# A bias tile with its own place, four transpose tiles, a third raw buffer and an earlier weight load in a hybrid S5 and chunked-attention layer

## The chip, the cores and the metric

The kernel runs on one core of a Trainium2 chip. Its time is the device time of one execution in microseconds; the kernel before has a median of 2287.17 us over three runs (2282.82 to 2289.53). All data are float32. Large products are made as three products of operands that are split into a high and a low part ("hi" and "lo", type float32r).

The engines go by their short names: PE (TensorE, the matrix products), DVE (VectorE), ACT (ScalarE), POOL (GpSimd) and SP (SyncE, which issues most DMAs). Each engine takes its instructions in order. A DMA is issued by SP or by POOL and carried by the core's 16 DMA engines; a wait that stands before a DMA's issue holds up everything behind it on the issuing engine.

## The reference

One layer of a trunk with two parallel head groups over 2048 tokens and 1024 channels:

```python
h = rmsnorm(x, norm_mix_g)
proj = h @ w_in                      # u_ssm | q | k | v, 512 columns each
y_ssm = s5_mixer(u_ssm, ...)         # 32 groups of 16 channels, 64 complex states each, GLU
y_att = chunked_attention(q, k, v, rel_bias)   # 8 heads of 64, own chunk of 64 and 8 before it
mixed = concat(rmsnorm(y_ssm, g_ssm), rmsnorm(y_att, g_att))
x = x + mixed @ w_out
h2 = rmsnorm(x, norm_ffn_g)
x = x + (silu(h2 @ w_gate) * (h2 @ w_up)) @ w_down
return rmsnorm(x, norm_final_g)
```

The attention adds a learned bias to each score, `bias[h, clip(key - query, -128, 128)]`, masks keys outside the band, and takes the softmax. The S5 group is a diagonal complex state-space scan: discretised transition powers, input matrix and output matrix are worked out from the parameters, then the states are scanned along time.

## The kernel before

The work runs in stages: the projection of the S5 input `u` (`u_phase`, until about 110 us) with the scan's parameters (`ssm_prologue`) beside it; the attention with the S5 scan and then the mixing stage between its steps (`att_phase`); the rest of the mixing stage; gate and up; down. The change touches the seam from the first stage to the second.

**Order.** PE's matmuls and transposes are kept in the order in which the program writes them (`Ordered`). The instructions issued through `k.V`, `k.A` and `k.Q` (DVE, ACT, SP) keep their order among one another (`Pinned`). All others are placed by a planner at compile time: it takes the earliest written instruction that is ready in its own estimate of time, so that on SP or POOL a later written DMA can pass one that isn't ready. The order that it gives to each engine is then fixed, and the semaphore waits are made to fit.

**The seam.** In the order of the program:

- `u_phase` forms four blocks of `u` (groups of 24 matmuls `ps<-hi,wuh`), takes them out of PSUM into `us` tiles (`evac`, four buffers), and POOL stores these (`u<-us`, L517). Before the last block it calls `front[0]`, which starts the first query/key unit `qk_unit(0, 0)` and thereby loads weights 0 and 4, and after its first group `front[1]` (`operands`): `hT_unit(0)` loads and normalises the first 512 tokens, and `table` builds the bias table.
- The bias table `nbm` lies in DRAM: for each of 8 heads 128 rows of 640 values. SP issues one copy from DRAM to DRAM (`nbms<-nbs`, 2560 KB), in which each row is shifted by one value against the one above, and then two stores of a corner of 1e30 (`nbms<-corner`) for keys outside the band.
- The prologue then makes its pool `pk`: `bbg` (loaded from DRAM in pieces of 16 values, 64 bytes), four `vg` tiles, `kt`, and the tiles `bst`. With `bbg` and `vg` PE makes 64 small matmuls (`pp<-vg,bbg`), and after them 32 transposes (`transposes`), two to a PSUM tile `pp` (six buffers); ACT copies each into a `bst` tile, and POOL stores each of the four blocks (`bsts<-bst`, L319).
- Before these 64 matmuls PE runs the query/key product of the first head pair (`pf<-hi,w`), after the transposes the steps of the attention: scores (`sc`), the value product of the first half of the heads (`v_unit(0, 0)`, weights 8 and 10), the next pair's product `qk_unit(0, 1)` (weights 1 and 5), and the scan's units (`ssm_unit`).
- A weight of the first 512 tokens is loaded into a `raw` buffer and split into a `w` tile (three buffers) by ACT (hi, L177) and DVE (lo, L178); `keep_w` stores the split weight to DRAM for the later tokens (`wss<-w`).
- A score is taken from PSUM by one DVE instruction that adds the bias tile `nb` of its head and takes the minimum (L863). The first head's `nb` is loaded by SP where its first score is written, that of each next head at the third score of the one before.

**Memory.** The tiles of a pool lie upward from its lower end in the order in which they are first used. Of the pools on the right side, `aw` (the attention's operands and weights) lies at the end of memory, `uo` (the second set of operands, hi0o, lo0o, hi1o, ... of 2,048 bytes per partition, 32,768 in all) under it, and `u1` (the weights of `u`, small tiles, three `pb`, four `us`) under that. When `u_phase` ends, `pk` is laid where `uo` and `u1` were, with its upper end at the lower end of `aw`: five `kt` of 4,096 bytes, `bbg` 2,048, `dm` 2,048, four `vg` of 4,096, two `bst` of 4,096. A tile waits, one by one, for the last use of the tiles whose bytes it takes.

Of the kernel before, what the change touches and what calls it, by code (L numbers as in the profile page):

```python
# [16 lines left out]
P = 128  # L17
# [3 lines left out]
NG, CH, NS = 32, 16, 64  # L21
# [88 lines left out]
def f32(ap):  # L110
    return ap.bitcast(F32)
# [63 lines left out]
def split(k, hi, lo, raw, lo_eng=None, hi_eng=None):  # L175
    nc = k.nc
    (hi_eng or nc.scalar).copy(hi, raw)  # L177
    (lo_eng or nc.gpsimd).tensor_tensor(lo, raw, f32(hi), op=ALU.subtract)  # L178


def ssm_prologue(k, ident, S):

    tc, nc, io = k.tc, k.nc, k.io
    V = nc.vector
    with tc.tile_pool(name="pro", bufs=1) as p:
# [122 lines left out]
                eng.tensor_tensor(out, t1, t2, op=op)  # L308

        def transposes(pk, b_, wt):  # L310
            bst = k.t(pk, "bst", [P, 8, 2, NS], bufs=2)
            for q in range(4):
                ps = k.t(k.pro_psum, "pp", [P, 512])[:].rearrange("p (a b) -> p a b", a=4)
                for c in range(2):
                    k.te.transpose(ps[:, c, :], wt[c][:, q].rearrange("p j c -> p (j c)"), ident[:])
                nc.scalar.copy(bst[:, 2 * q : 2 * q + 2].rearrange("p g c n -> p c g n"), ps[:, :2].rearrange("p c (g n) -> p c g n", g=2))
                if q % 2:
                    yield
            nc.gpsimd.dma_start(S["bst"][b_], bst[:].rearrange("p g c n -> p (g c n)"))  # L319
# [82 lines left out]
        pk = k.pk()  # L402
# [26 lines left out]
        for b_ in range(4):  # L429
            yield from transposes(pk, b_, wts[b_])  # L430
# [267 lines left out]
def att_phase(k, ident, S):  # L698
    tc, nc, io = k.tc, k.nc, k.io
    with ExitStack() as cx:  # L700
        aw = tc.alloc_tile_pool(name="aw", reuse_waits="tile", bufs=1, side="right")
        hT, vts, qk, keep = {}, {}, {}, {}

        def load_w(sb, n):

            w = k.t(aw, "w", [P, 2, 1024], F32R, bufs=WB)
            if sb == 0:
                raw = k.t(aw, "raw", [P, 1024], bufs=2)
                pin = n in (0, 4)
                (k.Q if pin else nc.sync).dma_start(raw[:], io["w_qk"][n] if n < 8 else io["w_v"][n - 8])  # L710
                split(k, w[:, 0], w[:, 1], raw[:], k.V if pin else k.wlo_eng, k.A if pin else None)
                keep[n] = w
            else:
                nc.sync.dma_start(f32(w[:]), S["ws"][n])
            return w[:, 0], w[:, 1]
# [5 lines left out]
        def hT_unit(sb, q0=0, q1=KT):  # L721
            hi, lo = hT.setdefault(sb, ([], []))
            ts = slice(sb * SB, (sb + 1) * SB)
            xts = {}
            V, A, Q = (k.V, k.A, k.Q) if sb == 0 else (nc.vector, nc.scalar, nc.sync)

            def load(q):
                if q < q1:
                    x = RING[q] if sb == 0 and q < 2 * DB else None
                    xts[q] = k.t(aw, x, [P, SB]) if x else k.t(aw, "xt", [P, SB], bufs=XB)  # L730
                    Q.dma_start(xts[q][:], io["xt"][q * P : (q + 1) * P, ts])

            ahead = 2 if sb else KT
            for q in range(q0, q0 + ahead):
                load(q)
            def low(q):
                V.tensor_tensor(lo[q][:], xts[q][:], f32(hi[q][:]), op=ALU.subtract)

            for q in range(q0, q1):
                yield  # L740
                load(q + ahead)
                xt = xts[q]
                for v, n in zip(hT[sb], ("hi", "lo")):
                    v.append(k.t(aw, f"{n}{q}x" if q < DB and sb % 2 else f"{n}{q}", [P, SB], F32R))
                V.scalar_tensor_tensor(xt[:], xt[:], k.gm[:, q : q + 1], S["rsn"][:, ts], op0=ALU.mult, op1=ALU.mult)
                A.copy(hi[q][:], xt[:])  # L746
                if sb == 0 and q:
                    low(q - 1)
                if sb or q == KT - 1:
                    low(q)  # L750
            yield

        def qk_unit(sb, pr):
            ws = [load_w(sb, n) for n in (pr, 4 + pr)]
            yield
            hi, lo = hT[sb]
# [42 lines left out]
        def v_unit(sb, fh):  # L799
            ws = [load_w(sb, 8 + 2 * r + fh) for r in range(2)]  # L800
            yield
            for i in range(4):
                vts[4 * sb + i, fh] = k.t(pv, f"v{fh}", [P, H // 2, 2 * HD], F32R)
            hi, lo = hT[sb]
            for i in range(4):
                ps = k.t(pfs, "pf", [P, 256])
                ic = slice(i * P, (i + 1) * P)
                for q in range(KT):
                    cs = slice((q % 4) * 256, (q % 4 + 1) * 256)
                    wh, wl = (w[:, cs] for w in ws[q // 4])  # L810
                    k.ta.matmul(ps[:], hi[q][:, ic], wh, start=q == 0, stop=False)
                    k.ta.matmul(ps[:], hi[q][:, ic], wl, start=False, stop=False)
                    k.ta.matmul(ps[:], lo[q][:, ic], wh, start=False, stop=q == KT - 1)
                    if q % 2 and q < KT - 1:
                        yield
                if i == 0:
                    for r in range(2):
                        keep_w(8 + 2 * r + fh)
                vt = vts[4 * sb + i, fh]
                pv3 = ps[:].rearrange("p (h d) -> p h d", h=4)  # L820
                nc.scalar.copy(vt[:, :, :HD], pv3)
                nc.vector.tensor_tensor(vt[:, :, HD:], pv3, f32(vt[:, :, :HD]), op=ALU.subtract)
                yield
# [3 lines left out]
        class Head:  # L827
            pass

        nbs = {}  # L830

        def load_nb(h):
            nb = k.t(aa, "nb", [P, 640], bufs=2)
# [88 lines left out]
        def table():  # L922
            corner = k.t(aw, "corner", [64, 64])
            nc.gpsimd.memset(corner[:], 1e30)
            k.Q.dma_start(S["nbm"][:], bass.AP(S["nb"].tensor, S["nb"].offset + 1, [[768, H], [1, P], [1, 640]]))
            for m in range(2):
                k.Q.dma_start(S["nbm"][:, m * 64 : m * 64 + 64, m * 576 : m * 576 + 64].rearrange("h p c -> p h c"), corner[:].unsqueeze(1).to_broadcast([64, H, 64]))

        def operands():
            for _ in hT_unit(0):  # L930
                pass
            table()

        pro = u_phase(k, ident, S, aw, (lambda: next(first), operands))
        pfs = cx.enter_context(tc.tile_pool(name="apf", bufs=2, space=bass.MemoryType.PSUM, reuse_waits="tile"))
        pps = k.pro_psum = tc.alloc_tile_pool(name="apro", bufs=6, space=bass.MemoryType.PSUM, reuse_waits="tile")
# [711 lines left out]
def block_kernel(tc, io, phases="pusamf"):  # L1648
# [3 lines left out]
    with ExitStack() as cx:  # L1652
# [32 lines left out]
        with tc.tile_pool(name="powers", bufs=1) as p:  # L1685
            S["a8"] = k.t(p, "a8", [P, 2, NPR, 16])
            S["sw"] = k.t(p, "sw", [P, 3, 2, NPR])
            mix = att_phase(k, ident, S)
# [58 lines left out]
```

## Time and profile before

| | us |
|---|---|
| median of three runs | 2287.17 |
| the profiled execution | 2284.15 |
| its span, first to last instruction | 2282.4 |
| PE busy in the span | 2180.3 |
| first query/key product ends, 64 small matmuls begin | 121.24 |
| first score | 141.29 |
| second pair's query/key product begins | 160.08 |

A row of the timeline gives start and duration in us, engine, line of the kernel, operation, output and inputs by the program's names, the count of instructions merged into it, and in brackets the idle time of the engine before it with what ended it. A row of the waits gives who waited for whom, then total time, number and longest. A row of a table of stretches gives for each engine (PE, PEld, DVE, ACT, POOL) the busy time and in brackets the instructions, then the granted clock of PE as a share of full speed, the busy share of the DMA engines and GB/s. A row of the DMA issues gives the transfer, its count, KB each, and the median time from issue to landing.

### The profile page before, as it was taken

How to read it: one execution, taken by the hardware profiler on the slowest of the kernel's cores; microseconds unless marked ns; L12 is line 12 of the kernel's file. 1: busy time of each engine (PE TensorE's matmuls, PEld its weight loads, DVE VectorE, ACT ScalarE, POOL GpSimd, SP SyncE). 2: the span in 40 equal slices, each digit the busy share in tenths (PEclk: the TensorE clock that was granted, in tenths of full speed). 3: DMA queues.
4: the chain of work that ended last, by engine and by line, in shares of the span. 5: the costliest groups of instructions: out<-in, count | busy, mean ns of one | idle time of the engine just before them, and what ended most of it. 6: DMA issues, size and time to landing. Idle time of an engine off the chain costs nothing.

```text
span 2282.4 us, 30410 instructions
## 1 busy us (share of the span) xinstructions
PE 2180.3 (96%) x10576; PEld 1833.1 (80%) x10576; DVE 1480.2 (65%) x2253; ACT 999.0 (44%) x1686; POOL 1011.1 (44%) x1222
## 2 busy tenths in 40 slices
PE   8978899999997999999999999999999999999998
PEld 6767688898986788878888887788888878888887
DVE  7845555656548656776776659776646376579576
ACT  6335555555557552343333334433333343345322
POOL 3406645456651122145555555555555414345450
PEclk9989999999998999999999999999999999999999
DMA  8787776766645334844454557454523297565552
GB/s 300 262 285 264 221 219 192 217 201 194 198 129 172 134 124 149 281 157 152 162 193 161 205 187 269 152 209 165 175 88 120 75 334 266 173 212 194 184 212 75
DMA packets 215890, 437.26 MB, mean 192 GB/s; under 512 B 27448, under 2 KB 58216, under 8 KB 208632
## 3 DMA queue, kind: packets, MB, share of 16 engines
q1 hardware_dynamic: 209736, 417.74, 55.2%
q0 software_dynamic: 6000, 17.58, 2.4%
q8 instruction: 83, 1.36, 0.2%
q14 instruction: 71, 0.58, 0.1%
HBM read 294.98 MB, written 132.41 MB: 187 GB/s over the span
## 4 chain that ended last, share of the span: by engine, by line
PE 77%; DVE 8%; issue 5%; DMA 4%; POOL 3%; ACT 2%; SPq 1%; DVEq 0%; POOLq 0%; ACTq 0%
PE ps L77 20%; PE X L77 18%; PE Y L77 9%; PE big L77 9%; PE pf L77 8%; PE W L77 4%; PE pj L77 4%; PE pt L80 2%; PE sc L77 2%; DMA xt<-in_xt 1%; DVE lo L178 1%; SPq L579 1%; DVE S L1407 1%; DVE acc L1617 1%; DVE cm L91 0%
## 5 line engine op out<-in xcount | busy, mean ns | idle before, releaser
L77 PE MATMUL X<-hi,c 128*128 128x512 f32 x1408 | 452.3, 392 | 6.0 <-ACT u L1425 3.3
L77 PE MATMUL ps<-hd,hd 128*128 128x512 f32 (+1 forms) x1968 | 428.2, 379 | 2.0 <-DVE hd L178 2.0
L77 PEld LDWEIGHTS ps<-hd,hd 128*128 128x128 f32 x1968 | 356.4, 188 | 72.4 <-DVE hd L178 3.1
L178 POOL TENSOR_TENSOR c<-S,c 128x512 fp32r<-128x512 f32 x172 | 249.4, 1452 | 263.1 <-ACT c L177 259.1
L77 PEld LDWEIGHTS X<-hi,c 128*128 128x128 f32 x1408 | 265.8, 189 | 64.4 <-ACT u L1425 5.3
L77 PE MATMUL X<-lo,c 128*128 128x512 f32 x704 | 275.4, 391 | 0.0
L178 POOL TENSOR_TENSOR hd<-hd 128x1536 fp32r<-128x1536 f32 (+1 forms) x46 | 156.3, 3401 | 216.1 <-ACT hd L177 204.6
L177 ACT CAST hd<-hd 128x1536 fp32r<-128x1536 f32 (+1 forms) x106 | 147.2, 1393 | 215.8 <-DMA hd<-hq 158.0
L178 POOL TENSOR_TENSOR c<-raw,c 128x512 fp32r<-128x512 f32 x129 | 184.2, 1428 | 128.2 <-ACT c L177 95.5
L77 PE MATMUL Y<-hi,c 128*128 128x512 f32 x704 | 225.6, 390 | 7.7 <-DVE u L1429 7.7
L1556 DVE TENSOR_TENSOR acc<-acc,ps 128x512 f32<-128x512 f32 x196 | 129.2, 681 | 75.0 <-PE ps L77 74.7
L77 PE MATMUL big<-m,woh 128*128 128x512 f32 x512 | 162.8, 400 | 0.0
L77 PEld LDWEIGHTS Y<-hi,c 128*128 128x128 f32 x704 | 132.5, 188 | 37.4 <-DVE u L1429 9.8
L177 ACT CAST c<-S 128x512 fp32r<-128x512 f32 x176 | 109.4, 622 | 115.3 <-PE Y L77 56.5
L77 PE MATMUL pf<-hi,w 128*128 128x512 f32 x416 | 150.9, 415 | 7.1 <-ACT hi L746 3.7
L77 PEld LDWEIGHTS X<-lo,c 128*128 128x128 f32 x704 | 133.0, 189 | 27.6
L1425 ACT COPY u<-X 128x512 f32<-128x512 f32 x132 | 77.2, 585 | 169.7 <-PE X L77 169.7
L863 DVE CUSTOM_DVE_ANT_0 s<-sc,nb 128x640 f32<-128x640 f32 (+4 forms) x128 | 94.4, 738 | 84.8 <-PE sc L77 80.7
L617 POOL TENSOR_TENSOR st<-X,a 128x128 f32<-128x128 f32 (+2 forms) x136 | 46.8, 344 | 231.3 <-ACT X L603 193.0
L177 ACT CAST c<-raw 128x512 fp32r<-128x512 f32 x132 | 82.1, 622 | 139.8 <-PE Y L77 78.6
L178 DVE TENSOR_TENSOR hd<-hd 128x1536 fp32r<-128x1536 f32 (+1 forms) x60 | 117.9, 1966 | 34.0 <-ACT hd L177 33.3
L77 PE MATMUL Y<-lo,c 128*128 128x512 f32 x352 | 137.3, 390 | 0.0
(468 smaller groups left out, 4605.0 us busy)
## 6 DMA issues: line engine op xcount, KB each, us to landing
w<-wss SPq DMA_DIRECT2D x36, 1024.0 KB, 5.9
hq<-g SPq DMA_DIRECT2D x133, 256.0 KB, 2.1
hd<-hq SPq DMA_DIRECT2D x42, 768.0 KB, 4.6
hd<-wc SPq DMA_DIRECT2D x42, 768.0 KB, 6.0
raw<-in_w_gate SPq DMA_DIRECT2D x44, 512.0 KB, 3.7
raw<-in_w_up SPq DMA_DIRECT2D x44, 512.0 KB, 4.0
wc<-px SPq DMA_DIRECT2D x66, 256.0 KB, 3.5
wss<-w SPq DMA_DIRECT2D x12, 1024.0 KB, 5.4
```

The lines of the kernel that those rows point to most:

```text
L77: return self.tc.keep_in_program_order(self.tc.nc.tensor.matmul(*a, **b))
L80: return self.tc.keep_in_program_order(self.tc.nc.tensor.transpose(*a, **b))
L177: (hi_eng or nc.scalar).copy(hi, raw)
L178: (lo_eng or nc.gpsimd).tensor_tensor(lo, raw, f32(hi), op=ALU.subtract)
L579: ins = nc.sync.dma_start(out, in_)
L617: eng.tensor_tensor(t[:, :, :, :n], src, ar, op=ALU.mult)
L863: nc.vector.tensor_tensor_reduce(s[:, :nk].rearrange("p (a b) -> p a b", a=nch), ps[:, :nch, :half], hd.nb[:, nk - 1 :: -1].rearrange("p ( ...
L1407: V.tensor_tensor(o[:], x, y, op=op)
L1425: nc.scalar.copy(u[:], ps[:])
L1556: V.tensor_tensor(a, a, ps[:], op=ALU.add)
L1617: nc.vector.scalar_tensor_tensor(v, v, k.go[:, i : i + 1], rs, op0=ALU.mult, op1=ALU.mult)
```

## The change

- `transposes` gets four `bst` buffers in place of two.
- `raw` gets three buffers in place of two, and its loads get a function of their own, `load_raw`. In `operands`, SP now issues the loads of weights 8 and 10 ahead of the bias table, and that of weight 1 between the table's copy and its two corner stores. All three are kept in SP's written order; before, they were placed by the planner where the weights are split.
- The first head's bias tile gets a place of its own, `nb0`, in a pool at the left side that lives as long as the attention, and is loaded by POOL right behind the table. The other heads' tiles are loaded as before.

```diff
         def transposes(pk, b_, wt):
-            bst = k.t(pk, "bst", [P, 8, 2, NS], bufs=2)
+            bst = k.t(pk, "bst", [P, 8, 2, NS], bufs=4)
...
         hT, vts, qk, keep = {}, {}, {}, {}
+        nb0 = k.t(cx.enter_context(tc.tile_pool(name="nb0", bufs=1)), "nb0", [P, 640])
+        raws = {}
+        def load_raw(n, dma):
+            raw = raws[n] = k.t(aw, "raw", [P, 1024], bufs=3)
+            dma(raw[:], io["w_qk"][n] if n < 8 else io["w_v"][n - 8])
...
             if sb == 0:
-                raw = k.t(aw, "raw", [P, 1024], bufs=2)
                 pin = n in (0, 4)
-                (k.Q if pin else nc.sync).dma_start(raw[:], io["w_qk"][n] if n < 8 else io["w_v"][n - 8])
+                if n not in raws:
+                    load_raw(n, (k.Q if pin else nc.sync).dma_start)
+                raw = raws.pop(n)
...
-        nbs = {}
+        nbs = {0: nb0}
...
             k.Q.dma_start(S["nbm"][:], bass.AP(S["nb"].tensor, S["nb"].offset + 1, [[768, H], [1, P], [1, 640]]))
+            load_raw(1, k.Q.dma_start)
             for m in range(2):
                 k.Q.dma_start(S["nbm"][:, ...], corner[:]...)
...
             for _ in hT_unit(0):
                 pass
+            for n in (8, 10):
+                load_raw(n, k.Q.dma_start)
             table()
+            nc.gpsimd.dma_start(nb0[:], S["nbm"][0])
```

The pool `pk` thereby takes 57,344 bytes per partition in place of 49,152, and `aw` 4,096 more.

## The prediction

> **What bounds the kernel now.** I read the page first, then the waits of PE in the stretch that the diff touches, then that stretch in order of time on each engine, and last the landing times of its transfers. The page says that PE is the bound over the whole:
>
> ```profile
> span 2282.4 us, 30410 instructions
> PE 2180.3 (96%) x10576; PEld 1833.1 (80%) x10576; DVE 1480.2 (65%) x2253; ACT 999.0 (44%) x1686; POOL 1011.1 (44%) x1222
> PE 77%; DVE 8%; issue 5%; DMA 4%; POOL 3%; ACT 2%; SPq 1%; DVEq 0%; POOLq 0%; ACTq 0%
> ```
>
> PE is idle for some 102 us in all (2282.4 - 2180.3), and its matmuls run in the order written. Time is won only where PE waits or runs slowly, and what is won early stays won while nothing behind it is tied to a fixed moment. Between 120 and 420 us it has three single waits over 3 us. Two lie in the stretch of the change and stand in brackets below; the third lies behind it, at 184 us (total, times, longest):
>
> ```profile
> PE pf L77 <- ACT w L177: 3.4, 1, 3.4
> ```
>
> In order of time on PE, from the end of the first query/key product to the start of the second:
>
> ```profile
> 121.24 7.27 PE L77 MATMUL pp<-vg,bbg 128*16 128x128 f32 x64
> 128.44 3.68 PE L80 MATMUL pp<-ident,vw 128*128 128x128 f32 x28
> 139.25 1.11 PE L80 MATMUL pp<-ident,vw 128*128 128x128 f32 x4 [7.13 <-ACT bst L316]
> 141.29 0.48 PE L77 MATMUL sc<-hi2x,hi0x 128*128 128x128 f32 x1 [0.93 <-ACT bst L316]
> ...
> 151.11 0.55 PE L77 MATMUL sc<-hi2x,hi0x 128*128 128x256 f32 x1 [4.21 <-DVE mn L863]
> ...
> 157.12 0.48 PE L77 MATMUL pf<-w,hi 128*128 128x256 f32 x2
> ...
> 160.08 0.40 PE L77 MATMUL pf<-hi,w 128*128 128x512 f32 x1
> ```
>
> From 121.24 to 160.08 PE spends 38.84 us. The 7.13 us wait is the third transpose tile: ACT stands before it until the first tile's store has landed. The 4.21 us wait is the first score, which needs its bias table:
>
> ```profile
> 129.43 2.21 ACT L316 COPY bst<-pp 128x256 f32<-128x256 f32 x8
> ...
> 138.82 0.92 ACT L316 COPY bst<-pp 128x256 f32<-128x256 f32 x3 [4.50 <-DMA bsts<-bst]
> ```
>
> ```profile
> 150.67 0.29 DVE L863 CUSTOM_DVE_ANT_0 s<-sc,nb 128x128 f32<-128x128 f32 x1 [2.89 <-DMA nb<-nbms]
> ```
>
> Both waits also cost clock. In these stretches of 2 us the third value from the right is the granted clock of PE:
>
> ```profile
> 132.00:134.00 2.00, 0.12 (x2) 0.00 (x0) 0.00 (x0) 0.72 (x1) 0.47 (x1) 1.00 1.04 371
> 136.00:138.00 2.00, 0.00 (x0) 0.00 (x0) 0.00 (x0) 0.00 (x0) 0.00 (x0) 0.54 1.03 413
> 146.00:148.00 2.00, 0.91 (x6) 0.70 (x5) 0.42 (x1) 0.37 (x1) 0.00 (x0) 0.90 0.94 233
> ```
>
> PE stops at about 132.1, is at half clock from about 136, and is back at about 146.4, some 7 us after it went on at 139.25. After the second wait it went on at 151.11, and the full-speed group of value products begins at 157.1, some 6 us later.
>
> **The change part by part.** What it can remove, first. At full clock the same stretch needs: the 64 small matmuls, 7.2 us (121.24 to 128.44); 32 transposes at 3.68/28 = 0.131 us, 4.2; the gap from the last transpose to the first score, which waits for the last bst copies to free the PSUM bank, 0.9; three scores with three groups of 24 value matmuls. One such group at full clock ran from 157.12 to 160.08, 2.96 us, with its scores before it about 0.35, so 3 x 3.3 = 9.9. Together 22.2. So at most 38.84 - 22.2 = 16.6 us can go: 7.1 by the four transpose tiles, 4.2 by the early bias tile, 5.3 by the clock and small gaps.
>
> *Four transpose tiles* remove the 4.50 us wait of ACT and with it PE's 7.13, since four blocks then have four tiles. What is late next is PSUM: six buffers, emptied by ACT at 2.21/8 = 0.28 us for two transposes (0.26 us of PE), so they keep step.
>
> *The bias tile by POOL.* Before, it stands on SP behind two weight stores that wait for a split:
>
> ```profile
> 93.22 0.80 SPq L91 DMA_DIRECT2D nbms<-nbs  x1
> 106.22 0.39 SPq L408 DMA_DIRECT2D bbg<-bbs  x1
> 106.93 9.58 SPq L415 DMA_DIRECT2D vg<-vs  x1
> 116.61 1.37 SPq L91 DMA_DIRECT2D nbms<-corner  x2
> 118.19 3.35 SPq L415 DMA_DIRECT2D vg<-vs  x3
> 121.59 2.00 SPq L91 DMA_DIRECT2D wss<-w  x2
> 123.63 2.31 SPq L710 DMA_DIRECT2D raw<-in_w_v  x2
> ...
> 135.61 6.68 SPq L719 DMA_DIRECT2D wss<-w  x2
> 142.38 0.72 SPq L834 DMA_DIRECT2D nb<-nbms  x1
> ```
>
> On POOL it waits only for the two corner stores (issued by 118 us, landing 4.4 us later by the row below). With one more landing, 8 us at the busy place where it now stands, it is there at about 131, ahead of any first score.
>
> ```profile
> nbms<-corner SPq DMA_DIRECT2D x2, 128.0 KB, 4.4
> ```
>
> ```profile
> nb<-nbms SPq DMA_DIRECT2D x1, 320.0 KB, 8.0
> ```
>
> It costs one POOL issue of about 0.5 us. What queues behind it on POOL are the kt and bst stores, from 127 us on, so this is covered if the planner puts it after the `us` stores (else see the third rival).
>
> *Third raw buffer, and the three weight loads moved.* The value weights (8, 10) now go ahead of the bias table, weight 1 (the second pair's query weights) between table and corners. SP loses 2.31 us of issue at 123.63. The value weights were loaded behind the first weight stores; now they come some 30 us earlier, so with the other waits gone they aren't the next stall. Their price is 1.5 MB more in the rings before the corners, of which 1 MB stands ahead of the table. At the 219 GB/s of the next row (last value) that is up to 4.8 us of delay for the table and the corners:
>
> ```profile
> 100.00:110.00 10.00, 10.00 (x44) 8.04 (x43) 9.91 (x17) 3.80 (x7) 0.56 (x2) 1.00 0.65 219
> ```
>
> The corners were issued at 116.61 only because the issue of the first vg took 9.58 us, so that delay is largely hidden; uncovered it would move vg 2 to 4, which land just in time now, by as much.
>
> *What the larger bst moves in memory.* This is the term that speaks against the change. `pk` lies directly under `aw`, where `uo` and `u1` lay. By the sizes in the code it was 49,152 bytes per partition and becomes 57,344, and its tiles are laid upward from its lower end. Before, bbg begins 28,672 bytes below the end of `pk`: that is hi1o. It waits for the second q of the last `us` group, and is issued at 106.22, vg one q (three matmuls, 0.7 us) later, as the rows show. After, bbg begins 36,864 below: above the 32,768 bytes of `uo`, in the four `us` tiles at the end of `u1`. It must then wait until a `us` tile has been stored. These rows are POOL's first three stores of the last group, and the landings of issues from 105 to 112 us:
>
> ```profile
> 109.38 1.74 POOL L517 DMA_DIRECT2D u<-us  x3 [10.46 <-DVE us L91]
> ```
>
> ```profile
> u<-us POOLq DMA_DIRECT2D x4, 256.0 KB, 5.1
> vg<-vs SPq DMA_DIRECT2D x1, 512.0 KB, 13.6
> bbg<-bbs SPq DMA_DIRECT2D x1, 256.0 KB, 11.8
> ```
>
> The quickest vg load (minimum, median and maximum of four) and the weight stores:
>
> ```profile
> DMA to landing us min/median/max: 4.9/5.6/13.6
> ```
>
> ```profile
> wss<-w SPq DMA_DIRECT2D x12, 1024.0 KB, 5.4
> ```
>
> The tile in question is the third to be stored: issue about 110.6, landing 115.7. Then bbg goes out, 4,096 pieces of 64 bytes. Its landing is bounded below by vg's quickest (4.9 us, 120.6: no stall at all) and above by its own 11.8 behind two 1 MB weight stores (their landing is 5.4 us, so 132.9). I take its own 11.8 us: 127.5. The vg loads, whose tiles now lie on the first q of `uo`, come earlier and aren't the limit. The 64 matmuls then start at 127.5 and not at 121.24: 6.3 us of a new wait. It is longer than the 4 us after which the clock fell at 132 to 136, so about 6.3 us behind it (the mean of 7 and 5.6) run at half speed, 3.1 more. New cost 9.4 us.
>
> The Trainium skill ("TensorE: Matmul & The Clock Gate", Part 1) gives about 3.4 us for the idle time that halves the clock and about as much sustained work to restore it. The first is near this trace (4), the second shorter than its 6 to 7. By the page the clock after the new wait would cost an estimated 1.7 us in place of 3.1, and the sum would be -8.6.
>
> *Sum.* 16.6 - 9.4 = 7.2 us less. Against the profiled execution's own 2284.15 us (its span 2282.4 and 1.75 around it) that makes 2276.9; the median shown, 2287.17, lies 3.0 above that execution, so **2280.0** for the median. Downstream I cost nothing: the first SSM unit's loads stand on SP behind the store of weight 1, whose split waited for a load that is now early, so they move up with the products.
>
> **The rivals.** *First: bbg costs nothing, or a later wait goes too.* If bbg lands by about 122, the whole 16.6 us stay: 2270.6. Or the third raw buffer lets the weights of the third pair load earlier and takes away the wait of PE for them (3.4 us by the row of the waits, plus clock). For: those pieces shared the rings with 1 MB of `us` stores when they took 11.8. Against: they will share them with vg.
>
> *Second: the gain is eaten up.* The planner sees bbg late and issues the two stores of weights 0 and 4 ahead of it. It lands at 132.9; the stall is 11.7 and 3.1 of clock, and 1.8 us are left: 2285.4. For: SP is in order, those stores are ready, and 106 to 116 is empty otherwise. Against: they stand behind the corners, which wait for the table.
>
> *Third, slower: the bias tile's load stands ahead of the `us` stores on POOL.* It waits there for the corners. These issue at 116.61 and land at about 121; then POOL issues it, then the third `us` store, landing about 127.2, then bbg after 11.8 at 139.0. Stall 17.8 and 3.1 of clock against 16.6: 4.3 slower, 2291.5; with the two stores ahead 9.7 slower, 2296.9. It decides from the point where bbg lands after 134.7 (121.24 + 16.6 - 3.1). Against: the `us` stores are earlier in the program and ready earlier. For: nothing holds POOL's order by hand.
>
> *That the change doesn't do what it says*: the first score could still wait for the doubled query rows, issued now from 126 on. That is inside the second rival's time.
>
> **How the numbers follow.** Forecast (3 to 12 us less) 0.42; first rival 0.24; second 0.20; third 0.14. About 0.3%, 6.9 us, is what a measurement can tell from no change. The forecast's middle lies at that bound, so somewhat over half of it counts as faster: 0.24 + 0.24 = 0.48. Slower beyond the bound is two thirds of the third rival and a little of the second, 0.12. The rest, 0.40, is no change. The range goes from below the first rival's time, with a later wait gone too (2267), to the third rival's near value (2291).
>
> **What would show it.** No wait of pp for bst; bbg issued after 115 us and not at 106; an idle PE of about 6 us before the small matmuls; the first scores without a wait for mn; the second pair's product starting at about 153 and not at 160.08, and the units behind it earlier by as much. I am wrong if bbg is issued before 110 or lands before 122, if PE stands before the first score for another operand, or if the 7 us are there at 160 and gone by the end of the attention.

## The result, and the profile after

The changed kernel takes 2280.53 us (median of 22 runs, 2272.24 to 2285.84); the kernel before, run beside it as often, takes 2284.93 us (2277.26 to 2291.03). The ratio is 0.9979 with a 95% interval of [0.997, 0.9989]: 4.4 us less by the medians (2.5 to 6.9 by the interval). The interval excludes a ratio of 1, but the gain is small beside the spread of the runs (13.6 us after, 13.8 before). The profiled execution took 2283.70 us, so it is one of the longer ones. The page after has the shape of the page before:

```profile
span 2281.9 us, 30399 instructions
PE 2183.0 (96%) x10576; PEld 1834.0 (80%) x10576; DVE 1482.7 (65%) x2253; ACT 996.6 (44%) x1686; POOL 1010.4 (44%) x1223
PE 75%; DVE 8%; DMA 6%; issue 4%; POOL 2%; SPq 2%; ACT 2%; DVEq 0%; POOLq 0%; ACTq 0%
```

PE in order of time, kernel after, the rows that answer to those from 121.24 to 160.08 before:

```profile
111.20 0.47 PE L77 MATMUL pf<-hi,w 128*128 128x512 f32 x1 [1.36 <-DVE us L91]
...
126.44 9.82 PE L77 MATMUL pp<-vg,bbg 128*16 128x128 f32 x64 [4.10 <-DMA vg<-vs]
136.19 4.53 PE L80 MATMUL pp<-ident,vw 128*128 128x128 f32 x32
141.07 0.33 PE L77 MATMUL sc<-hi2x,hi0x 128*128 128x128 f32 x1 [0.35 <-ACT bst L316]
145.65 0.36 PE L77 MATMUL sc<-hi2x,hi0x 128*128 128x256 f32 x1 [1.22 <-DVE mn L871]
152.17 0.40 PE L77 MATMUL pf<-hi,w 128*128 128x512 f32 x1
```

The transposes run through (32 in one row), the 7.13 us wait for `bst` is gone, and of the 4.21 us at the first bias tile 1.22 are left. A new wait of 4.10 us stands at the 64 small matmuls, and these take 9.82 us in place of 7.27. The second pair's product starts at 152.17, that is 7.91 us earlier (160.08 - 152.17). The issues of SP show where the new wait comes from:

```profile
92.73 1.69 SPq L91 DMA_DIRECT2D raw<-in_w_v  x2
94.47 0.79 SPq L91 DMA_DIRECT2D nbms<-nbs  x1
95.36 9.77 SPq L91 DMA_DIRECT2D raw<-in_w_qk  x1
118.21 0.38 SPq L408 DMA_DIRECT2D bbg<-bbs  x1
118.70 2.94 SPq L91 DMA_DIRECT2D nbms<-corner  x2
121.81 4.45 SPq L415 DMA_DIRECT2D vg<-vs  x4
```

The waits of SP there, and the stores that end the longest one (POOL, then their landing in the last column):

```profile
SPq L408 <- DMA u<-us: 12.8, 1, 12.8
```

```profile
111.35 2.33 POOL L517 DMA_DIRECT2D u<-us  x4 [12.92 <-DVE us L91]
```

```profile
u<-us POOLq DMA_DIRECT2D x4, 256.0 KB, 5.4
```

So `bbg` does wait for a `us` tile to be stored, as predicted, and is issued 12 us later than before. But the operand that PE then waits for is `vg`. Before, its first load was issued at 106.93, ahead of the corner stores; now the planner has put all four behind them, at 121.81. In this kernel the corners show no wait of their own: they are issued as soon as `bbg` is out, at 118.70, and take 2.94 us. The clock answers as before (third value from the right):

```profile
122.00:124.00 2.00, 0.35 (x2) 0.00 (x0) 1.93 (x4) 0.93 (x2) 0.00 (x0) 1.00 0.64 132
124.00:126.00 2.00, 0.00 (x0) 0.00 (x0) 1.93 (x4) 0.00 (x0) 0.57 (x1) 0.78 1.09 322
126.00:128.00 2.00, 1.56 (x8) 1.12 (x9) 1.97 (x4) 0.59 (x1) 0.00 (x0) 0.50 1.14 376
...
130.00:132.00 2.00, 2.00 (x12) 1.37 (x10) 0.28 (x1) 0.82 (x2) 0.54 (x1) 0.52 1.15 431
132.00:134.00 2.00, 2.00 (x20) 1.78 (x19) 0.28 (x1) 1.23 (x3) 0.02 (x1) 1.00 0.98 410
```

Both traces hold the same 10,576 matmuls in the same order, so the start of one matmul can be set against the same matmul before. I call the difference the lead (minus is earlier) and the time in the kernel before its mark; a lead is taken at the last matmul that starts before the mark. The lead after is +1.0 us at mark 120, -7.9 at 160, -7.8 at 210, -3.6 at 235, +2.4 at 425, -4.0 at 970 and 0.0 at the last matmul. So in this execution the seam's gain is gone at the end, though the medians keep 4.4 us of it. The experiments take the seam apart first, and then ask where the rest went.

### The profile page after: what moved, and what is told of

Same layout as the page of the kernel before. It is cut to its first block, busy times and chain, and to the rows that moved or that the text cites. A ratio compares the mean times of both kernels' runs of the same rounds, so it can differ in the third digit from the quotient of the medians.

```text
span 2281.9 us, 30399 instructions
## 1 busy us (share of the span) xinstructions
PE 2183.0 (96%) x10576; PEld 1834.0 (80%) x10576; DVE 1482.7 (65%) x2253; ACT 996.6 (44%) x1686; POOL 1010.4 (44%) x1223
## 3 DMA queue, kind: packets, MB, share of 16 engines
q8 instruction: 83, 1.36, 0.2%
## 4 chain that ended last, share of the span: by engine, by line
PE 75%; DVE 8%; DMA 6%; issue 4%; POOL 2%; SPq 2%; ACT 2%; DVEq 0%; POOLq 0%; ACTq 0%
PE ps L77 20%; PE X L77 18%; PE Y L77 9%; PE pf L77 8%; PE big L77 7%; PE W L77 4%; PE pj L77 4%; PE pt L80 2%; PE sc L77 2%; DMA xt<-in_xt 1%; DVE lo L178 1%; DMA bsts<-bst 1%; DMA lo<-hc 1%; SPq L579 1%; DVE acc L1629 1%
## 5 line engine op out<-in xcount | busy, mean ns | idle before, releaser
L77 PEld LDWEIGHTS Y<-hi,c 128*128 128x128 f32 x704 | 132.9, 189 | 37.9 <-DVE u L1441 10.2
```

What stands on the lines that cost most here:

```text
L77: return self.tc.keep_in_program_order(self.tc.nc.tensor.matmul(*a, **b))
```

## The experiments

The experiments ran in three groups, each with the kernel before beside it on the same chip; its medians were 2283.5, 2285.72 and 2284.69 us, and each ratio is against the runs of before in the same group. Leads come from one profiled execution per kernel.

| kernel | ratio, 95% interval | bbg issued | waits at the 64 matmuls | lead at 160 | at 235 |
|---|---|---|---|---|---|
| after | 0.9979 [0.997, 0.9989] | 118.21 | 4.10 | -7.9 | -3.6 |
| after, run again | 0.9988 [0.9969, 1.0006] | 119.38 | 5.20 | -7.1 | -4.6 |
| before + four bst tiles | 0.9995 [0.9981, 1.0008] | 112.69 | 1.68 | -5.0 | -5.0 |
| before + early bias tile | 0.9989 [0.9974, 1.0003] | 105.05 | 1.72 | -6.1 | -5.5 |
| after, two bst tiles | 1.0039 [1.0025, 1.0052] | 105.44 | 3.70 | +3.2 | +8.6 |
| after without the early weight loads, bst apart | 0.9975 [0.9961, 0.9989] | 107.07 | 1.59 | -11.0 | -3.4 |
| after, bst apart | 0.9977 [0.9963, 0.9991] | 107.38 | 3.16 | -8.9 | -6.6 |
| after, corners late | 0.998 [0.9965, 0.9994] | 119.47 | 3.17 | -9.2 | -3.7 |
| after, bst apart, corners late | 0.9967 [0.9951, 0.9983] | 107.80 | 0.83 | -11.0 | -6.2 |
| the last, first scan unit a step longer | 0.9955 [0.9939, 0.9971] | 106.78 | 0.96 | -11.0 | -9.7 |

**The kernel after, unchanged, once more.** No edit; it tells how far one profile can be trusted.

> The changed kernel once more, for a second profile of it. My theory: what the seam does is fixed by the program (bbg issued at 118 +- 1.5 us, PE idle about 4 us before the 64 small matmuls, second pair's product begun at 152 +- 1.5 us), while what the units behind it give back varies from execution to execution. So the seam should look the same and the lead over the kernel before at the end should differ by some us from the 0.5 us of the first profile. The rival, that the 7 us are given back by a fixed chain behind the seam (the scan's first unit: XG), expects the same loss at the same places: at 217 to 230 us and at 400 to 417 us. Time: 2280 +- 4 us.

Its time was 2281.86 us. The seam repeats: the second pair's product within 0.8 us (lead -7.1 at 160), the issue of bbg (119.38) and the wait for vg (5.20) within 1.2. The loss between 210 and 235 is there again too (-9.6 to -4.6), as the rival expected for its first place; its second, at 400 to 417 us, doesn't repeat. The lead at mark 425 is -3.2 here, where it was +2.4. Single leads behind the first scan unit thus move by several us from one execution to the next, and I read nothing from them alone.

**Four transpose tiles alone.**

```diff
 # in the kernel before
-            bst = k.t(pk, "bst", [P, 8, 2, NS], bufs=2)
+            bst = k.t(pk, "bst", [P, 8, 2, NS], bufs=4)
```

> The kernel before with four bst tiles and nothing else. Theory: the larger pk alone moves bbg onto a us tile; it is issued at 115 +- 1.5 us and not at 106, PE waits 3 to 7 us before the 64 small matmuls, the 7.1 us wait between the transposes is gone, the 4.2 us wait at the first scores stays. Second pair's product at 157 to 161 us; total within 4 us of the kernel before. Rival (the late bbg of the changed kernel comes from the earlier weight loads): bbg at 106 us, no wait before the small matmuls, second pair's product at about 152.

PE, kernel before with four tiles:

```profile
119.17 1.91 PE L77 MATMUL pp<-vg,bbg 128*16 128x128 f32 x16 [0.31 <-DMA vg<-vs]
122.44 5.42 PE L77 MATMUL pp<-vg,bbg 128*16 128x128 f32 x48 [1.37 <-DMA vg<-vs]
127.79 3.82 PE L80 MATMUL pp<-ident,vw 128*128 128x128 f32 x32
136.07 0.45 PE L77 MATMUL sc<-hi2x,hi0x 128*128 128x128 f32 x1 [4.46 <-DMA hi0x<-hi0x]
147.01 0.55 PE L77 MATMUL sc<-hi2x,hi0x 128*128 128x256 f32 x1 [5.64 <-DVE mn L863]
```

The memory step of the prediction is seen by itself: this one number moves the issue of bbg from 106.22 to 112.69. But the small matmuls start at 119.17, so bbg has landed at most 6.5 us after its issue, not 11.8, and PE waits 1.68 us there, not the 3 to 7 expected. And the 7.13 us gained at the transposes are partly taken by the next waits: 4.46 for the doubled query rows, 5.64 in place of 4.21 for the bias tile. Of the lead of -5.0 at mark 160, -2.3 stand at mark 75 already, ahead of anything edited, so the tiles alone win about 2.5 us in the seam. The time is that of the kernel before within the interval.

**The early bias tile alone.**

```diff
 # in the kernel before
+        nb0 = k.t(cx.enter_context(tc.tile_pool(name="nb0", bufs=1)), "nb0", [P, 640])
...
-        nbs = {}
+        nbs = {0: nb0}
...
+            nc.gpsimd.dma_start(nb0[:], S["nbm"][0])   # behind the corner stores
```

> The kernel before, with the first head's bias tile in a place of its own, loaded by POOL; two bst tiles, two raw buffers and the weight loads as before. Theory (the parts of the sum are separate): the first score's wait for its minimum (4.2 us before) goes, the wait of the transposes for bst (7.1 us) stays, bbg is issued at about 106, the second pair's product starts 4 to 6 us earlier than before, the time is 3 to 5 us under before's. Rival (the two waits cover each other): behind the wait for bst another wait takes the place of the one removed, for weights or the doubled query rows, the second pair's product starts less than 2 us earlier and the time is before's within 1.5 us.

PE, kernel before with the early bias tile:

```profile
139.37 1.12 PE L80 MATMUL pp<-ident,vw 128*128 128x128 f32 x4 [6.93 <-ACT bst L316]
141.41 0.47 PE L77 MATMUL sc<-hi2x,hi0x 128*128 128x128 f32 x1 [0.93 <-ACT bst L316]
147.49 0.36 PE L77 MATMUL sc<-hi2x,hi0x 128*128 128x256 f32 x1 [1.22 <-DVE mn L864]
```

The wait for `bst` stays, that for `mn` falls to 1.22. The 1.22 us stand in nearly every kernel with the early tile, so they aren't the tile: the second score group waits for DVE to take the first. The product is 6.1 us earlier, 1.2 of it from ahead of the seam. The ratio (-2.5 us, -5.9 to +0.7) does not tell the theory from its rival; the trace speaks for the theory.

**After, with two transpose tiles.**

```diff
 # in the kernel after
-            bst = k.t(pk, "bst", [P, 8, 2, NS], bufs=4)
+            bst = k.t(pk, "bst", [P, 8, 2, NS], bufs=2)
```

> The changed kernel with two bst tiles again, all else kept. Theory: pk has its old size, bbg lies over hi1o, is issued by 107 us; the wait of ACT for the store of the first bst tile is back, and PE waits 5 to 9 us for it between the transposes; no wait for the bias tile at the first scores. Second pair's product at 154 +- 2.5 us, total 2 to 4 us above the changed kernel. Rival (the order on SP holds vg): as well a wait for vg of 2 to 4 us, so 157 +- 2 us and no gain left against the kernel before.

```profile
124.85 8.77 PE L77 MATMUL pp<-vg,bbg 128*16 128x128 f32 x64 [3.70 <-DMA vg<-vs]
149.33 1.11 PE L80 MATMUL pp<-ident,vw 128*128 128x128 f32 x4 [10.89 <-ACT bst L316]
```

This is PE with all of the change but the tiles. The loads moved up make the seam worse: 3.70 us at the small matmuls although bbg is issued at 105.44, and 10.89 at the transposes in place of 7.13. The kernel is 8.9 us slower than before (ratio 1.0039, 5.7 to 11.9 us). Both sides expected less: the second pair's product starts at 163.29, later than the 157 of the rival, whose wait for vg is there. So the rest of the change gains nothing without the four tiles, as these alone gained nothing clear, and the vg wait is there without bbg's new place. On SP the corners stand ahead of all four vg loads here as well (114.85, vg from 120.45), although bbg is early; with four tiles alone, where bbg is late, the first vg is still ahead of them (113.25, corners 115.78). So the new order on SP goes with the early weight loads and not with the late bbg.

**Without the early weight loads.** Four tiles in a pool of their own (so that bbg lies over `uo` again, on hi3o where it lay on hi1o before) and the early bias tile, on the kernel before; two raw buffers, weights loaded where they are split.

```diff
 # in the kernel before
-            bst = k.t(pk, "bst", [P, 8, 2, NS], bufs=2)
+            bst = k.t(pk, "bst", [P, 8, 2, NS], bufs=4)
...
+        pb = tc.alloc_tile_pool(name="pb4", bufs=1, side="right", reuse_waits="tile")
...
-            yield from transposes(pk, b_, wts[b_])
+            yield from transposes(pb, b_, wts[b_])
+        pb.release()
...
+            nc.gpsimd.dma_start(nb0[:], S["nbm"][0])   # with nb0 as above
```

> The kernel before, with four bst tiles in a place of their own and the first bias tile by POOL, but without the third raw buffer and without the early loads of weights 8, 10 and 1. Set beside the kernel with the place alone (0.9977 of before), it differs only by those loads. Theory (the early loads put 1.5 MB ahead of the corners and cost the vg wait, and buy nothing by themselves): bbg at about 106, vg wait under 1.5 us, the second pair's product 10 to 14 us ahead of the kernel before, the time 1 to 4 us under the kernel with the place alone. Rival (the early loads are needed): without them the value product or the second pair's product waits for its weight by 3 us or more behind the first scores, the second pair's product starts within 2 us of the kernel with the place alone or later, and the time is the same or higher.

PE, this kernel:

```profile
123.71 3.67 PE L77 MATMUL pp<-vg,bbg 128*16 128x128 f32 x32 [1.10 <-DMA vg<-vs]
...
152.01 0.51 PE L77 MATMUL pf<-hi,w 128*128 128x512 f32 x1 [2.77 <-ACT w L177]
```

Both sides were partly right. Without the loads the seam up to the second pair's product is as short as in the best kernel below (-11.0 at 160, though a wait of 4.09 us for the doubled query rows stands in it). Yet this product then waits 2.77 us for its weight, starts at 152.01, 8.1 us earlier than before, and runs at half speed at first; by mark 175 the lead is -6.0. The 1 to 4 us that the theory expected in the time aren't there: it is that of the kernel with the loads and bst apart (0.9975 and 0.9977, intervals of 0.14% to either side). As far as these tell, the early loads buy behind the seam about what they cost in it.

**bst in a place of its own.** Now the new wait, first the place in memory.

```diff
 # in the kernel after
+        pb = tc.alloc_tile_pool(name="pb4", bufs=1, side="right", reuse_waits="tile")
...
-            yield from transposes(pk, b_, wts[b_])
+            yield from transposes(pb, b_, wts[b_])
+        pb.release()
```

> The changed kernel with the four bst tiles in a pool of their own under pk, so that bbg lies over hi3o and lo3o again and not over a us tile. Theory 1 (the larger bst, by its place in memory, holds bbg and all that stands behind it on SP): bbg is issued at 106 to 108 us and not at 118, PE's wait for vg (4.1 us) falls under 1 us, the clock stays full, and the second pair's product begins at 146 +- 1.5 us; total some 4 to 7 us under the changed kernel, if nothing gives it back. Rival (the earlier weight loads and the new order on SP, with the corners ahead of all four vg, hold vg): bbg is early but the corners still wait for the table's copy until about 115 to 118, vg is issued at 118 to 120 and PE still waits 2 to 4 us; second pair's product at 149 to 152; total within 3 us of the changed kernel.

SP and PE of this kernel:

```profile
107.38 0.38 SPq L409 DMA_DIRECT2D bbg<-bbs  x1
115.47 5.12 SPq L91 DMA_DIRECT2D nbms<-corner  x2
120.81 4.56 SPq L416 DMA_DIRECT2D vg<-vs  x4
```

```profile
125.49 8.81 PE L77 MATMUL pp<-vg,bbg 128*16 128x128 f32 x64 [3.16 <-DMA vg<-vs]
```

bbg is back at 107.38, so its delay was the memory place. PE still waits 3.16 us: the four vg loads stand behind the corners, and these now wait for the landing of the table's copy. The wait of SP for it:

```profile
SPq L91 <- DMA nbms<-nbs: 7.7, 1, 7.7
```

The rival foretold this, with its product at 149 to 152 (151.18). With the place mended, what is left of the wait is SP's order.

**The corners behind the vg loads.**

```diff
 # in the kernel after: table() returns the corner tile, and what follows it moves
-            table()
-            nc.gpsimd.dma_start(nb0[:], S["nbm"][0])
+            keep["corner"] = table()
...
         pro = u_phase(k, ident, S, aw, (lambda: next(first), operands))
+        corners(keep.pop("corner"))     # the two corner stores, then nb0's load by POOL
```

> The kernel after, with the table's two corner stores and the load of the first bias tile moved in program order behind the loads of bbg and the four vg tiles; memory and all else as after. Theory (the vg loads stood behind the corners, and these behind the landing of the table's copy): bbg is issued at about 118 as before, the vg loads follow it at once, the 64 small matmuls wait about 2 us for vg in place of 4.1 to 5.2, the corners are issued at about 123 and the first bias tile lands at about 133, ahead of the first score; the second pair's product starts 1.5 to 3 us earlier than after (at about 150), the time is 0 to 3 us under after's. Rival 1 (bbg's own lateness by the memory place is the stall): the wait at the small matmuls stays at 4 to 5 us and only changes its name from vg to bbg, the time is after's within 1 us. Rival 2: the bias tile is late, the first score waits 3 us or more for its minimum (mn), and the time is 2 to 4 us over after's.

bbg at 119.47, the vg loads from 120.02, a wait of 3.17 us: about 1 us better than after (and 2 better than its second run), as with bst apart, where the theory had expected about 2 us of wait. Neither repair alone is enough, as long as either the place or the order holds vg until 120.

**Both repairs.** The two edits above together.

> Both repairs: four bst tiles in a place of their own, so that bbg takes the place it had before, and the corners with the bias tile's load behind bbg and vg. Theory (place and order each give a part of the new wait, and together they are all of it): bbg issued at about 107, the vg loads right behind it, no wait over 1 us at the 64 small matmuls, clock full through them, the second pair's product at 146 to 148 (12 to 14 us ahead of the kernel before), the time 3 to 6 us under the kernel with the place alone (2277.6 in its run, here 0.9977 of the kernel before). Rival 1 (a lead won in the seam is given back at the scan's first unit, whose XG waits for its own loads): the lead at the seam is 12 us or more, yet at the mark 225 us it is 8 or less, as with the place alone, and the time is the same as with the place alone within 1.5 us. Rival 2: the bias tile, now behind the kt stores on POOL, makes the first score wait for its minimum by 3 us or more.

SP and PE of this kernel:

```profile
107.80 0.38 SPq L409 DMA_DIRECT2D bbg<-bbs  x1
108.51 15.00 SPq L416 DMA_DIRECT2D vg<-vs  x4
123.62 2.77 SPq L91 DMA_DIRECT2D nbms<-corner  x2
```

```profile
123.56 7.39 PE L77 MATMUL pp<-vg,bbg 128*16 128x128 f32 x64 [0.83 <-DMA vg<-vs]
...
137.50 0.30 PE L77 MATMUL sc<-hi2x,hi0x 128*128 128x128 f32 x1 [1.79 <-DMA hi0x<-hi0x]
...
149.05 0.40 PE L77 MATMUL pf<-hi,w 128*128 128x512 f32 x1
```

The wait is 0.83, the 64 matmuls take 7.39 us at full clock, and the product starts at 149.05, 11.0 us ahead of the kernel before (1.1 later than I expected; a wait of 1.79 us for the query rows and a lead of +1.4 at mark 120, ahead of the seam, stand against it). So place and order together are the new wait. The time, 0.9967, is a little lower than with one repair (the theory had 3 to 6 us less), but the intervals overlap, and of the lead of -10.5 at mark 210 4.3 us are gone at mark 235: the first rival, that the lead is given back while the scan's first unit ends, holds in the trace.

**The scan's copies left out.** After the seam PE waits for XG, four copies that POOL issues when the scan's first unit is done. After, in order of time:

```profile
215.01 0.67 PE L77 MATMUL pj<-XG,Vm 128*128 128x256 f32 x2 [1.67 <-DMA XG<-X]
...
217.53 1.19 PE L77 MATMUL pj<-XG,Vm 128*128 128x256 f32 x2 [1.41 <-DMA XG<-X]
```

The second run of after waits once, and longer:

```profile
215.73 1.19 PE L77 MATMUL pj<-XG,Vm 128*128 128x256 f32 x2 [3.85 <-DMA XG<-X]
```

The granted clock in the first run:

```profile
216.00:220.00 4.00, 2.59 (x7) 2.06 (x7) 0.69 (x1) 0.91 (x2) 0.00 (x0) 0.66 0.57 160
```

The same matmul in the kernel before:

```profile
221.59 0.67 PE L77 MATMUL pj<-XG,Vm 128*128 128x256 f32 x2 [1.53 <-DMA XG<-X]
```

The landing of these copies, the first row before, the second after:

```profile
XG<-X POOLq DMA_DIRECT2D x4, 127.5 KB, 4.9
```

```profile
XG<-X POOLq DMA_DIRECT2D x4, 127.5 KB, 6.6
```

POOL's chain has moved up with the seam (first copy issued at 204.20 in place of 211.72), but the copies take longer to land, PE stands twice, and the granted clock falls to 0.66. In the second run the copies land in 5.2 us, but POOL's first copy is only 6.7 us earlier than before (205.00), where PE's lead is 9.6. Three kernels (before, after, and both repairs) without the copies:

```diff
 # for the first unit only
-        nc.gpsimd.memset(k.XG[:, :, 0:1], 0.0)
+        nc.gpsimd.memset(k.XG[:], 0.0)
...
-    for g2 in range(2):
+    for g2 in range(2 if b else 0):
```

> The kernel before, with the four copies of the scan's states into XG left out for the first scan unit (XG is set to zero instead; so the first quarter of the S5 output lacks the carried states). It is the yardstick for the two runs beside it. Theory (the lead of the seam is given back where PE stands for these copies): of the kernel before only the one wait of 1.53 us at 221.59 us goes; the time is 1 to 2 us under before's (ratio about 0.9993). Rival (the copies weigh on other things too, such as the rings): the time moves by 4 us or more.

> The kernel after, with the same four copies left out. Theory: the two waits for XG (1.67 and 1.41 us) and the stretch at a granted clock of 0.66 behind them go, the lead of 7 to 9 us that stands at the mark 210 us of the kernel before is still 7 to 8 at the mark 235 (it was 3.6), and the time is about 7 us under that of the kernel before with the copies left out, and 3.5 to 5 us under after's. Rival (the lead leaks away anyway, at the next place that has its own clock, since the scan's pace and the loads are what they were): the lead at 235 is as large, but by 430 us it is 4 or less, and the time is only 3 to 5 us under that of the kernel before with the copies left out.

> The kernel with both repairs (four bst tiles in a place of their own, corners and first bias tile behind bbg and vg), with the same four copies left out. Theory: its lead of 10 to 11 us at the mark 210 us is 9 to 10 at 235 (it was 6.2), and the time is 8 to 10 us under that of the kernel before with the copies left out. Rival (leak further on): 9 to 10 at 235, 6 or less from 430 us on, the time 4 to 6 us under that of the kernel before with the copies left out.

| without the copies | us | ratio to before, 95% interval | lead at 210 | at 235 | at 425 | at the end |
|---|---|---|---|---|---|---|
| before | 2280.17 | 0.9976 [0.996, 0.9992] | -3.0 | -4.9 | -2.4 | -2.8 |
| after | 2276.17 | 0.9954 [0.9938, 0.9971] | -9.8 | -9.3 | -7.5 | -6.0 |
| both repairs | 2271.77 | 0.9945 [0.9923, 0.9968] | -10.7 | -10.3 | -7.6 | -10.5 |

Against the kernel before, the lead of the kernel after stays at -9.3 with the copies gone, and that of both repairs at -10.3. But the yardstick moved too, and its own waits for XG are gone as well. Against the kernel before without the copies, the lead of after falls from -6.9 at 210 to -4.4 at 235, and that of both repairs from -7.7 to -5.4: 2.4 to 2.5 us, where 4.2 to 4.3 went with the copies. So in these profiles less than half of the loss there goes with the copies. The kernel with bst apart says the same: in its profile PE doesn't stand for XG at all, and its lead still falls from -10.0 to -6.6. What takes the rest isn't shown.

In the times, the kernel before gains 4.5 us by the same edit (1.8 to 9.1 by the interval), against 1 to 2 expected, and its own profile shows only 1.9 us of that at the place (-3.0 to -4.9; -2.4 us of its lead are there at mark 75 already, ahead of anything edited). Between before and after there remain 4.0 us without the copies and 4.4 with them. Both repairs lie 8.4 us under the kernel before without the copies, inside the theory's 8 to 10, but with the copies they lay 7.0 us under it, and the difference is inside the intervals. So the theory that the give-back at XG is why the total shows less than the seam isn't borne out by the times. The rival, a leak further on, foretold the 3 to 5 us, but its sign, a lead of 4 or less by mark 430, isn't in the trace of after (-7.5 at 425). Where the rest goes is open.

**A version with slack.** Both repairs, and the first scan unit ends one attention step later, the second begins one later.

```diff
-  Unit(ssm_unit(...), SSM_N, 2 + int(SW * b), 2 + int(SW * (b + 1)), light=SL)
+  Unit(ssm_unit(...), SSM_N, 2 + int(SW * b) + (b == 1), 2 + int(SW * (b + 1)) + (b == 0), light=SL)
```

> The kernel with both repairs, the whole computation; the first scan unit ends one attention step (about 4.4 us) later and the second begins one later. Theory: the copies into XG have landed when PE comes to them, no wait for XG over 0.5 us, the lead at the mark 235 us is 9 to 10 us (it was 6.2), and the time is 3 to 4 us under the kernel with both repairs (2278.7 beside 2285.7, ratio 0.9967), that is a ratio of about 0.995. Rival (the wait only moves: the second unit's loads need the first unit's tiles, and start one step later): PE waits 2 us or more for U at the second unit's first product, or for XG at its end some 60 us later, and the time is that of the kernel with both repairs within 1.5 us.

PE, this kernel, first and second scan unit:

```profile
214.45 0.67 PE L77 MATMUL pj<-XG,Vm 128*128 128x256 f32 x2 [0.54 <-DMA XG<-X]
215.76 0.67 PE L77 MATMUL pj<-XG,Vm 128*128 128x256 f32 x2 [0.20 <-DMA XG<-X]
```

```profile
281.99 1.19 PE L77 MATMUL pj<-XG,Vm 128*128 128x256 f32 x2 [2.79 <-DMA XG<-X]
```

The time is 2274.73 us, ratio 0.9955: about 10 us under before, the lowest median of the kernels that do the whole work, and under both kernels of this case. At the first unit it went almost as the theory said (0.54 and 0.20 us, lead -9.7 at 235; this kernel has the scan's matmuls at other places in PE's order, so its leads count only where the orders meet, as they do at the marks given). At the second the rival's wait appears, 2.79 us. Its interval overlaps that of both repairs without the step (0.9967), so what the step itself is worth isn't settled.

## Why the prediction was right or wrong

**The number.** Forecast were 2280.0 us and 7.2 us less; measured were 2280.53 and 4.4 less. That the time was met within 0.5 us is luck: the gain is 2.8 us smaller than forecast, and the starting point 2.2 us lower (the three runs shown had a median of 2287.17, the 22 beside the result 2284.93). The measured gain lies in the forecast's band of 3 to 12 us; the 7.2 us themselves lie just outside the measured interval (2.5 to 6.9).

**The seam, by its steps.**

- *Four transpose tiles, 7.1 us:* right. The wait is gone and PE doesn't stand for PSUM. That the gain needs the tiles is shown by the run with two of them, which is slower than before; that they aren't enough, by the run with the tiles alone (0.9995).
- *The early bias tile, 4.2 us:* 3.0 of it. The floor of 22.2 us left out the 1.22 us that a score group waits for DVE.
- *bbg on a `us` tile:* the mechanism was right (waiting for `u<-us`, and 112.69 by four tiles alone). The issue was put at 115.7 and came at 118.21. Of these 2.5 us, 2 come from POOL's stores, which start at 111.35 and not at 109.38, because DVE does an early weight's split ahead of the last norms and `us` tiles:

```profile
100.26 1.23 DVE L178 TENSOR_TENSOR w<-raw,w 128x1024 fp32r<-128x1024 f32 x1 [1.34 <-ACT w L177]
```

  That is a price of the early loads which the prediction did not have. PE's 1.36 us wait at 111.20 is its trace, and the lead of +1.0 ahead of the seam. In all nine profiles of kernels with the early loads the lead changes by +0.3 to +1.5 us between marks 75 and 120, in the four others by at most 0.15.
- *Its landing, 11.8 us, stall 6.3:* mis-sized. bbg took at most 8.2 us after (118.21 to 126.44), at most 6.5 with four tiles alone, and PE waited 4.10.
- *"The vg loads ... come earlier and aren't the limit":* this step failed. PE waits 4.10 us for vg. I followed bbg's bytes and left SP's order as it was, but the planner put all four vg loads behind the corners. In the kernel after these follow bbg, so that vg is late by bbg's wait of 12.8 us and the 2.94 us of the corners; with bbg early they wait for the table's copy instead, and vg is hardly earlier (120.81). bst apart left 3.16 us, corners late 3.17, both together 0.83.
- *The clock, 3.1 us:* 2.55, at the small matmuls (9.82 - 7.27). The transposes took 0.3 more than the 4.2 I gave them, but at full clock. The Trainium skill ("TensorE: Matmul & The Clock Gate", Part 1) gives about 3.4 us of sustained work for the way back to full speed, and the estimate from it was 1.7; in the kernel after the way back took 5.5 us (126.44 to 131.9), with bst apart 3.6 (125.49 to 129.1).
- *Sum:* the product was put at about 153 and starts at 152.17. Inside the seam the gain is 8.9 us (from +1.0 to -7.9), 1.7 more than forecast: the new wait and its clock cost 6.65 us (4.10 and 2.55) in place of 9.4, against the 1.22 that the floor left out. 1.0 is lost ahead of the seam.

**"Downstream I cost nothing."** This failed. The medians keep 4.4 of 7.9 us. The scan's chain on POOL did move up with the products, as I had argued. But in the profiles 4 to 5 us go while the scan's first unit ends (-7.8 to -3.6, and -9.6 to -4.6 in the second run), where PE waits for the copies and the clock falls. The kernels without the copies put less than half of this down to the copies, and their times don't confirm that they are why the total shows less. Where the rest goes stays open. The sign I had named for being wrong, 7 us there at 160 and gone later, is what the profile after shows, and what the medians show in part.

**The rivals.** The first (2270.6) asked for bbg to land by about 122, and it was issued at 118.21, with vg behind it. Its other half, that a later wait goes too, didn't come: PE waits 3.42 us for the third pair's weight at 176.57, as it did before at 184.49. The second's time (2285.4) wasn't met; its cause, two weight stores ahead of bbg, isn't in SP's rows. The third put the bias tile's load ahead of the `us` stores; it is issued at 124.04, behind them:

```profile
124.04 0.57 POOL L944 DMA_DIRECT2D nb<-nbms  x1 [6.99 <-DMA nbms<-corner]
```

The wait of the first score for the doubled query rows isn't in the kernel after, but it is in four of the others (4.46, 4.09, 1.79 and 1.48 us).

## What to carry to other kernels

A tile count changes addresses, and an address changes who waits: lay out the pools' bytes before and after. Then also ask how a planner reorders the queue around loads that are moved, because the load that ends last may be another one. Loads that are moved up have a price on the engine that converts them and on the in-order queue behind them; here, as far as the intervals tell, it ate what they bought. And a lead won at one place is only worth what the next wait for a transfer leaves of it, so it should be followed past the change, in more than one execution, before it is counted.

## What the hardware showed that was not expected

- One issue of a plain 512 KB load took 9.77 us on SP behind the 2560 KB copy from DRAM to DRAM. With both repairs the four vg loads took 15.00 us to issue from 108.51 on, against 4.45 for the same four at 121.81 in the kernel after. Everything behind them on SP waited as long. What holds such an issue isn't shown.
- PE stopped at about 122.35 (0.35 us of work in the stretch from 122). A mean clock of 0.78 from 124 to 126 means half speed from about 125.1, 2.8 us after it stopped, where I had read 4 us from the stretch before.
- Worked out in this way, the half speed lasted 6.8 us here (125.1 to 131.9; the clock from 130 to 132 is 0.52), 10.2 us in the kernel before (136.2 to 146.4, from the 0.54 and 0.90 of its stretches) and 3.4 us with bst apart (125.7 to 129.1; 0.92 from 124 to 126, 0.72 from 128 to 130): one, two or three times 3.4 us. So the same 64 matmuls lose 2.55 us to the clock in the kernel after and 1.54 with bst apart (8.81 - 7.27), though the waits ahead of them differ by less than 1 us.
- Executions of one kernel differ behind the seam by more than the change is worth: +2.4 and -3.2 us of lead at mark 425, in two profiles of the same program.
